# Projections of an mLSTM layer: two column blocks at a time, half of the k chunks by Strassen's seven products

## The chip, the core and the metric

The kernel runs on one core of one Trainium2 chip. Time is microseconds of device time for one execution; three runs of the kernel before took 1814.03 to 1814.68 us, median 1814.12. The engines that matter here are PE (TensorE, the matrix products), DVE (VectorE), ACT (ScalarE), and SP, whose queue issues the loads.

## The reference

One layer: RMSNorm, an input projection, a chunkwise mLSTM mixer with 8 heads, gates, an output projection. All inputs are float32, 256 rows of 4096 columns.

```
u = h @ w_in                                   # [256, 4096] @ [4096, 16400]
qk, v, og, z, ig, fg = split(u)                # 4096, 4096, 4096, 4096, 8, 8 columns
qk = silu(causal_dwconv(qk, conv_w, conv_b))   # 4 taps over time
... per head: hc = the gated matrix memory of q, k, v, normed by rows
y = hn * sigmoid(og) * silu(z)
out = x + y @ w_out                            # [256, 4096] @ [4096, 4096]
```

The two projections hold nearly all of the arithmetic. The mixer itself is small: a head has 256 rows, 256 columns of q and of k and 512 of v.

## The kernel before, in words

A float32 product is made of three passes of a faster format. `split` (L127) makes of an operand a high part (ACT, L129) and a low part (DVE, L130), and `matmul3` (L132) adds high by high, high by low and low by high into one PSUM bank: three products of 512 columns, about 0.4 us each in the profile and overlapping, for one k tile (128 of the 4096 rows of w) and one row tile (128 of the 256 rows).

`project` (L165) takes one block of 512 columns at a time. It walks over 8 chunks of 4 k tiles. A chunk of w is one load of 1 MB (L188, three buffers); two k tiles at a time are split (128x1024, tiles `wh`, `wl`, three buffers each) and give 12 products: 2 k tiles, 2 row tiles, 3 passes. x lies split in SBUF for the whole layer. Work on finished blocks (convolution, attention weights, values, gates) lies in `stages`, and one stage is issued behind each chunk of the blocks that follow. The first two blocks run together while x comes in. Blocks of a pair of heads come in the order og, z, og, z, q, k, v, v; then 9 blocks of w_out.

The order of instructions on each engine is the tile scheduler's, which also puts in the waits; a buffer is written again only when its last reader is done. Names in rows: `pj_o` is a PSUM tile of block o, `w_o` a raw load, `wh_o` and `wl_o` its high and low part.

## Time and profile before

| | |
|---|---|
| three runs, median | 1814.12 us |
| span of the profiled execution (its own time, first to last instruction) | 1812.6 us |
| PE busy | 1805.7 us, 100% of the span |
| DVE busy | 965.0 us, 53% |
| ACT busy | 848.8 us, 47% |
| loads and stores | 354.07 MB, mean 195 GB/s |

The span is 1.5 us under the median of the runs. Busy time of PE counts overlapping products once. Idle time of an engine off the chain of waits costs nothing.

### The profile page before, as it was taken

Reading aid. Unit: us, or ns where it says so; the run is one execution under the profiler, and the core shown is the slowest. Engines: PE = TensorE matmul, PEld = TensorE weight load, DVE = VectorE, ACT = ScalarE, POOL = GpSimd, SP = SyncE. Lnnn points to the kernel's source line nnn. Section 1 sums busy time; section 2 is a strip of 40 time slices with the busy share of each in tenths; the row PEclk is TensorE's granted clock in tenths of the full one; section 3 lists DMA queues with packets and bytes.
Section 4 is the critical chain, followed back from the end, with each engine's and each line's share of the span. In section 5 each row is a group of like instructions: output and inputs, shape, how many; then the busy total and the mean of one; then the engine's idle time right before and its main releaser. Section 6 shows DMA issues by size and latency. Waiting matters only on the chain.

```text
span 1812.6 us, 20931 instructions
## 1 busy us (share of the span) xinstructions
PE 1805.7 (100%) x8474; PEld 1510.6 (83%) x8474; DVE 965.0 (53%) x1133; ACT 848.8 (47%) x994; POOL 9.4 (1%) x24
## 2 busy tenths in 40 slices
...
GB/s 311 277 204 176 200 187 186 181 168 188 199 193 188 190 181 185 164 197 196 187 196 194 175 176 172 200 185 195 200 186 185 171 225 209 219 222 203 213 187 141
DMA packets 57089, 354.07 MB, mean 195 GB/s; under 512 B 6944, under 2 KB 8352, under 8 KB 18592
## 3 DMA queue, kind: packets, MB, share of 16 engines
...
HBM read 348.51 MB, written 4.19 MB: 195 GB/s over the span
## 4 chain that ended last, share of the span: by engine, by line
PE 99%; DMA 0%; SPq 0%; ACT 0%; DVE 0%; issue 0%
PE pj_v L135 7%; PE pj_o L136 6%; PE pj_o L134 6%; PE pj_o L135 6%; PE pj_v L136 6%; PE pj_v L134 6%; PE pj_og L135 6%; PE pj_og L134 6%; PE pj_og L136 6%; PE pj_z L135 6%; PE pj_z L136 6%; PE pj_z L134 6%; PE pj_k L135 3%; PE pj_k L134 3%; PE pj_k L136 3%; PE pj_q L135 3%
## 5 line engine op out<-in xcount | busy, mean ns | idle before, releaser
L130 DVE TENSOR_TENSOR wl_o<-w_o,wh_o 128x1024 fp32r<-128x1024 f32 x128 | 156.8, 1225 | 174.6 <-ACT wh_o L129 174.6
L129 ACT ACTIVATE wh_o<-w_o 128x1024 fp32r<-128x1024 f32 x128 | 135.8, 1061 | 206.8 <-PE pj_o L136 206.0
L130 DVE TENSOR_TENSOR wl_z<-w_z,wh_z 128x1024 fp32r<-128x1024 f32 x112 | 137.2, 1225 | 167.4 <-ACT wh_z L129 167.4
L130 DVE TENSOR_TENSOR wl_v<-w_v,wh_v 128x1024 fp32r<-128x1024 f32 x128 | 156.7, 1224 | 116.3 <-ACT wh_v L129 115.4
L135 PE MATMUL pj_o<-wl_o,yh 128*128 128x512 f32 (+1 forms) x576 | 210.5, 366 | 0.0
L136 PE MATMUL pj_o<-wh_o,yl 128*128 128x512 f32 (+1 forms) x576 | 210.5, 366 | 0.0
L130 DVE TENSOR_TENSOR wl_og<-w_og,wh_og 128x1024 fp32r<-128x1024 f32 x112 | 137.1, 1225 | 135.9 <-ACT wh_og L129 135.4
L129 ACT ACTIVATE wh_v<-w_v 128x1024 fp32r<-128x1024 f32 x128 | 135.6, 1060 | 154.6 <-PE pj_v L136 136.1
L135 PE MATMUL pj_v<-wl_v,xhi 128*128 128x512 f32 x512 | 202.4, 395 | 0.0
L136 PE MATMUL pj_v<-wh_v,xlo 128*128 128x512 f32 x512 | 199.9, 391 | 0.0
L129 ACT ACTIVATE wh_z<-w_z 128x1024 fp32r<-128x1024 f32 x112 | 118.8, 1061 | 169.5 <-PE pj_z L136 146.2
L129 ACT ACTIVATE wh_og<-w_og 128x1024 fp32r<-128x1024 f32 x112 | 118.8, 1060 | 160.7 <-PE pj_og L136 141.7
L134 PE MATMUL pj_o<-wh_o,yh 128*128 128x512 f32 (+1 forms) x576 | 193.3, 366 | 0.0
L134 PE MATMUL pj_v<-wh_v,xhi 128*128 128x512 f32 x512 | 183.7, 391 | 0.0
L135 PE MATMUL pj_og<-wl_og,xhi 128*128 128x512 f32 x448 | 175.0, 391 | 0.0
L136 PE MATMUL pj_og<-wh_og,xlo 128*128 128x512 f32 x448 | 174.4, 389 | 0.0
L135 PE MATMUL pj_z<-wl_z,xhi 128*128 128x512 f32 x448 | 174.3, 389 | 0.0
L136 PE MATMUL pj_z<-wh_z,xlo 128*128 128x512 f32 x448 | 174.3, 389 | 0.0
L134 PE MATMUL pj_og<-wh_og,xhi 128*128 128x512 f32 x448 | 158.3, 390 | 0.0
L134 PE MATMUL pj_z<-wh_z,xhi 128*128 128x512 f32 x448 | 156.1, 389 | 0.0
L136 PEld LDWEIGHTS pj_o<-wh_o,yl 128*128 128x128 f32 x576 | 108.7, 189 | 17.4
L134 PEld LDWEIGHTS pj_o<-wh_o,yh 128*128 128x128 f32 x576 | 108.7, 189 | 17.4
...
## 6 DMA issues: line engine op xcount, KB each, us to landing
...
w_o<-in_w_out SPq DMA_DIRECT2D x16, 512.0 KB, 3.5
```

The lines of the kernel that those rows point to most:

```text
L129: nc.scalar.activation(hi, src, AF.Copy)
L130: nc.vector.tensor_sub(lo, src, hi.bitcast(F32))
L134: nc.tensor.matmul(ps, a[0], b[0], start=first, stop=False)
L135: nc.tensor.matmul(ps, a[0], b[1], start=False, stop=False)
L136: nc.tensor.matmul(ps, a[1], b[0], start=False, stop=last)
```

## The change

Columns of w are now taken in pairs of blocks, 1024 columns by 256 rows: a 2x2 of blocks (two row tiles by two column blocks). In chunks 0, 2, 4 and 6 (`FAST`) the four k tiles are halved as well, and the 2x2 by 2x2 block product is formed by seven products of block sums instead of eight (the Winograd form). The sums on x's side (`F` in `build`, L190) are made once and kept; the sums on w's side are made anew for each pair, in place in the raw loads, on DVE (L246, L252, L255, L258). Each of the seven products `P1` to `P7` has its own PSUM bank for the whole pair. The other four chunks (`plain_steps`) go into four of these banks, so that the last combination, `combine` (L313), serves both: four copies on ACT (L321), seven sums of 128x512 on DVE (L322 to L328) at the end of each pair.

A step of a fast chunk has 6 products behind one split of 128x1024, a step of a plain chunk 12. A fast and a plain chunk together, which the steps interleave, are called a round below: 7 x 6 + 4 x 12 = 90 products, 11 splits and 4 sums of 128x1024; a pair has 4 rounds, and there are 19 pairs, 15 in w_in and 4 in w_out. In the kernel before, the same columns and chunks took 96 products and 8 splits.

Head 0's q, k, v and the gate columns (1040 columns) are projected plainly in a first part while x comes in; in its last chunks `build_x` (L219) loads x again and makes the 14 or 6 operand tiles of a chunk. Then follow the pairs oz0 (og and z of head 0), qkv1 (q, k, v of head 1), oz1, and so on to oz7, then o0 to o3. Finished heads are written to DRAM and read back during oz7 (`build_y`, L505), since the operands of x and of y share their place. The row norm goes into x's operands. Raw loads are 0.5 MB, seven buffers; `wh` and `wl` have three each, as before. The row sum of the weights, before a column of ones beside the values, is now 48 products of two columns.

```diff
-WARM = 8
-NPAIR = HEADS // 2
-OUT_BLOCKS = [NB] * 7 + [NB // 2] * 2
...
+FAST = (0, 2, 4, 6)
+ORDER = ("P1", "P3", "P2", "P5", "P7", "P6", "P4")
+TAGS = ORDER
...
+def block_pairs():
+    pairs = []
+    for h in range(HEADS):
+        if h:
+            pairs.append(("qkv", h, [(h * DQK, DQK), (QK + h * DQK, DQK)], [(O_V + h * DV, DV)]))
+        pairs.append(("oz", h, [(O_OG + h * DV, DV)], [(O_Z + h * DV, DV)]))
+    return pairs
...
+    def operand(name, src):
+        n = src.shape[-1]
+        hi = wpool.tile([P, RAW], F32R, name=f"wh_{name}", tag="whi")[:, :n]
+        lo = wpool.tile([P, RAW], F32R, name=f"wl_{name}", tag="wlo")[:, :n]
+        split(hi, lo, src)
+        return hi, lo
...
+    def load(name, w, off, n):
+        raw = wpool.tile([P, RAW], F32, name=f"w_{name}", tag="wraw", bufs=7)[:, :n]
+        nc.sync.dma_start(raw, source(w, off, n))
+        return raw
...
-    def project(name, w, off, widths, lhs, start=False, between=None, end=False):
-        """Column blocks of w side by side, from off on; returns the psum tiles of each."""
-        ps = [[pool.tile([P, NB], F32, name=f"pj_{name}_{b}_{t}", tag=tag)[:, :width] for t in range(NT)]
-              for b, (width, (pool, tag)) in enumerate(zip(widths, ((ps_pj, "pj"), (ps_n, "n"))))]
...
-                    hi = wpool.tile([P, SK, NB], F32R, name=f"wh_{name}_{b}_{c}_{k0}", tag="whi")
-                    lo = wpool.tile([P, SK, NB], F32R, name=f"wl_{name}_{b}_{c}_{k0}", tag="wlo")
-                    hi, lo = (u.rearrange("p a b -> p (a b)")[:, :n * width].rearrange("p (a b) -> p a b", a=n)
-                              for u in (hi, lo))
-                    split(hi, lo, raws[b].rearrange("p (a b) -> p a b", a=CK)[:, k0:k0 + n, :])
-                    order = [(j, t) for j in range(n) for t in range(NT)]
-                    for j, t in sorted(order, key=lambda jt: jt[1]) if end else order:
-                        matmul3(ps[b][t], a, (hi[:, j, :], lo[:, j, :]), c == 0 and k == 0,
-                                c == KT // CK - 1 and k == CK - 1)
...
+    def build(c, src):
+        if c in FAST:
+            flat = lhs_pool.tile([P, 2 * 7 * HK * P], F32R, name=f"lhs_{c}", tag=f"lhs{c}")
+            L = flat.rearrange("p (two s j t) -> p two s j t", two=2, s=7, j=HK)
+            a11, a12, a21, a22 = (src[:, j * HK:(j + 1) * HK, t * P:(t + 1) * P]
+                                  for t, j in ((0, 0), (0, 1), (1, 0), (1, 1)))
+            F = big(f"F_{c}", [P, 4, HK, P])
+            nc.vector.tensor_sub(F[:, 0], a21, a22)
+            nc.vector.tensor_sub(F[:, 3], a21, a11)
+            nc.vector.tensor_sub(F[:, 1], a11, F[:, 0])
+            nc.vector.tensor_sub(F[:, 2], a12, F[:, 1])
+            t0 = src[:, :, :P].rearrange("p (s j) t -> p s j t", s=2)
+            for s0, s1, v in ((0, 2, t0), (2, 3, a22.rearrange("p (s j) t -> p s j t", s=1)), (3, 7, F)):
+                for a in range(s0, s1):
+                    split(L[:, 0, a], L[:, 1, a], v[:, a - s0])
+            names = ("P1", "P2", "P4", "P5", "P6", "P3", "P7")
+            lhs[c] = {s: [[L[:, part, i, j, :] for part in range(2)] for j in range(HK)]
+                      for i, s in enumerate(names)}
...
+            flat = lhs_pool.tile([P, 2 * 3 * CK * P], F32R, name=f"lhs_{c}", tag=f"lhs{c}")
+            L = flat.rearrange("p (two s j t) -> p two s j t", two=2, s=3, j=CK)
+            F = big(f"F_{c}", [P, CK, P])
+            nc.vector.tensor_sub(F, src[:, :, :P], src[:, :, P:])
+            for i, v in enumerate((src[:, :, :P], src[:, :, P:], F)):
+                split(L[:, 0, i], L[:, 1, i], v)
+            lhs[c] = {s: [[L[:, part, i, j, :] for part in range(2)] for j in range(CK)]
+                      for i, s in enumerate(("T0", "T1", "D"))}
+    def build_x(c):
+        src = big(f"xn_{c}", [P, CK, T])
+        nc.sync.dma_start(src, xT[:, c * CK:(c + 1) * CK, :])
+        for j in range(CK):
+            k = c * CK + j
+            nc.vector.scalar_tensor_tensor(src[:, j, :], src[:, j, :], nw[:, k:k + 1], rstdB,
+                                           op0=OP.mult, op1=OP.mult)
+        build(c, src)
...
+    def fast_steps(name, w, off, c):
+        n = HK * NB
+        at = off + c * 4 * P * n
+        raw = {}
+        def made(s):
+            if s == "P1":
+                raw["11"] = load(f"{name}_{c}_11", w, at, n)
+            elif s == "P3":
+                raw["22"] = load(f"{name}_{c}_22", w, at + P * n, n)
+            elif s == "P2":
+                raw["21"] = load(f"{name}_{c}_21", w, at + 2 * P * n, n)
+            elif s == "P5":
+                if not DSUM:
+                    raw["12"] = load(f"{name}_{c}_12", w, at + 3 * P * n, n)
+                    nc.vector.tensor_add(raw["11"], raw["11"], raw["12"])
...
+                    nc.vector.tensor_add(raw["22"], raw["22"], raw["11"])
+            elif s == "P7":
+                if not DSUM:
+                    nc.vector.tensor_add(raw["12"], raw["12"], raw["22"])
+                if DSUM < 3:
+                    nc.vector.tensor_add(raw["21"], raw["21"], raw["11" if DSUM else "22"])
+            src = raw[{"P1": "11", "P3": "22", "P2": "21", "P5": "11", "P6": "11" if DSUM else "22",
+                       "P7": "22" if DSUM else "12", "P4": "21" if DSUM < 3 else "11"}[s]]
+            h = operand(f"{name}_{c}_{s}", src)
...
+            return [(s, [(lhs[c][s][j], b) for j, b in enumerate(by_k(h))])]
+        return [(c, lambda s=s: made(s), 1) for s in ORDER]
...
+    def plain_steps(name, w, off, c):
+        n = HK * NB
+        at = off + c * 4 * P * n
+        def made(i):
+            b = by_k(operand(f"{name}_{c}_{i}", load(f"{name}_{c}_{i}", w, at + i * P * n, n)))
+            return [(s, [(lhs[c][l][(i % 2) * HK + j], b[j]) for j in range(HK)])
+                    for s, l in ((("P3", "D"), ("P5", "T1")), (("P2", "T0"), ("P4", "T1")))[i // 2]]
+        return [(c, lambda i=i: made(i), 2) for i in range(4)]
...
+    def project_pair(name, w, off, between=None):
+        ps = {s: bank(f"{s}_{name}", s) for s in TAGS}
+        fast = [u for c in FAST for u in fast_steps(name, w, off, c)]
+        plain = [u for c in range(NCH) if c not in FAST for u in plain_steps(name, w, off, c)]
+        steps = sorted([((i + 0.5) / len(fast), u) for i, u in enumerate(fast)]
+                       + [((i + 1) / len(plain), u) for i, u in enumerate(plain)], key=lambda v: v[0])
+        total = len(fast) + 2 * len(plain)
+        uses = {s: len(FAST) * HK for s in TAGS}
+        for s in ("P2", "P3", "P4", "P5"):
+            uses[s] += (NCH - len(FAST)) * CK
+        seen = dict.fromkeys(TAGS, 0)
+        left = {c: 7 if c in FAST else 4 for c in range(NCH)}
+        done = popped = 0
+        for _, (c, make, cost) in steps:
+            for s, prods in make():
+                for a, b in prods:
+                    seen[s] += 1
+                    matmul3(ps[s], a, b, seen[s] == 1, seen[s] == uses[s])
+            left[c] -= 1
+            done += cost
+            if between is not None:
+                between(c if left[c] == 0 else None, done / total)
+            if done * NCH >= (popped + 1) * total:
+                popped += 1
+                if stages:
+                    stages.popleft()()
+        return ps
...
+    def combine(name, ps, xs=None):
+        A = work.tile([P, NT, NB], F32, name=f"A_{name}", tag="cA")
+        B = work.tile([P, NT, NB], F32, name=f"B_{name}", tag="cB")
+        p1 = work.tile([P, NB], F32, name=f"p1_{name}", tag="p1")
+        r7 = work.tile([P, NB], F32, name=f"r7_{name}", tag="r7")
+        tt = nc.vector.tensor_tensor
+        for dst, s in ((p1, "P1"), (B[:, 0], "P3"), (B[:, 1], "P5"), (r7, "P7")):
+            nc.scalar.activation(dst, ps[s], AF.Copy)
+        tt(A[:, 0], ps["P2"], p1, op=OP.add)
+        tt(B[:, 0], B[:, 0], B[:, 1], op=OP.add)
+        tt(p1, ps["P6"], p1, op=OP.subtract)
+        tt(r7, r7, p1, op=OP.add)
+        tt(B[:, 0], B[:, 0], p1, op=OP.add)
+        tt(B[:, 1], B[:, 1], r7, op=OP.add)
+        tt(A[:, 1], ps["P4"], r7, op=OP.subtract)
+        return A, B
...
+    def build_y(c):
+        src = big(f"yr_{c}", [P, CK, T])
+        nc.sync.dma_start(src, spill[c])
+        build(c, src)
...
+            for b in ((0,), (1, 2), (3, 4))[c - 5]:
+                build_x(b)
+    builds = deque((build_x, c) for c in range(5, NCH))
...
+    stages.extend([merged(gate_stages[0], conv[0]), merged(gate_stages[1], conv[1]), gate_stages[2],
+                   merged(gate_stages[3], hs[0])] + hs[1:])
...
+                f(b)
+            if n == len(pairs) - 1 and c is not None and c < HEADS - 1:
+                build_y(c)
+        ps = project_pair(f"{what}{h}", w_in, off, between)
+        off += D * 2 * NB
+        A, B = combine(f"{what}{h}", ps)
+        if what == "qkv":
+            for t in range(NT):
+                split(V[0][:, t, :], V[1][:, t, :], B[:, t, :])
+            hs, finish = head(h)
+            stages.extend(conv_qk(h, A) + hs)
+        else:
+            def gate_y(A=A, B=B, finish=finish):
+                sg = big("sg", [P, NT, NB])
+                nc.scalar.activation(A, A, AF.Sigmoid)
+                nc.scalar.activation(sg, B, AF.Sigmoid)
+                nc.vector.tensor_mul(B, B, sg)
+                nc.vector.tensor_mul(B, B, A)
+                finish(B)
+            gate_y()
+            stages.extend(turn(h))
...
-        ps, = project(f"o{n}", w_out, done * D, [width], ylist, end=n == len(OUT_BLOCKS) - 1)
...
+    for n in range(D // (2 * NB)):
+        cols = [slice((2 * n + i) * NB, (2 * n + i + 1) * NB) for i in range(2)]
+        ps = project_pair(f"o{n}", w_out, n * D * 2 * NB)
...
+        res = combine(f"o{n}", ps)
+        for i in (1, 0):
+            for t in range(NT):
+                nc.vector.tensor_add(xs[i][:, t, :], xs[i][:, t, :], res[i][:, t, :])
+                eng = nc.gpsimd if n < 3 else (nc.sync, nc.scalar)[t]
+                eng.dma_start(out[t * P:(t + 1) * P, cols[i]], xs[i][:, t, :])
```

Three places show how instructions move. First DVE, in the third block of w_out: before, its row holds only low parts (two to a load).

```order
L130 TENSOR_TENSOR wl_o2_0_1_0_11202<-w_o2_0_1_11199,wh_o2_0_1_0_11201 128x1024
L130 TENSOR_TENSOR wl_o2_0_1_2_11218<-w_o2_0_1_11199,wh_o2_0_1_2_11217 128x1024
L130 TENSOR_TENSOR wl_o2_0_2_0_11236<-w_o2_0_2_11233,wh_o2_0_2_0_11235 128x1024
L130 TENSOR_TENSOR wl_o2_0_2_2_11252<-w_o2_0_2_11233,wh_o2_0_2_2_11251 128x1024
L130 TENSOR_TENSOR wl_o2_0_3_0_11270<-w_o2_0_3_11267,wh_o2_0_3_0_11269 128x1024
L130 TENSOR_TENSOR wl_o2_0_3_2_11286<-w_o2_0_3_11267,wh_o2_0_3_2_11285 128x1024
```

Now the same engine in the third pair of w_out, at the start of a round (chunks 4 and 5; `P1` to `P7` are steps of the fast chunk 4, `_5_0` and `_5_1` the first two of the plain chunk 5; rows of L246, L255, L252 and L258 are the in-place sums).

```order
L135 TENSOR_TENSOR wl_o2_4_P1_13670<-w_o2_4_11_13667,wh_o2_4_P1_13669 128x1024
L135 TENSOR_TENSOR wl_o2_4_P3_13682<-w_o2_4_22_13679,wh_o2_4_P3_13681 128x1024
L246 TENSOR_TENSOR w_o2_4_11_13667<-w_o2_4_11_13667,w_o2_4_12_13721 128x1024
L255 TENSOR_TENSOR w_o2_4_12_13721<-w_o2_4_12_13721,w_o2_4_22_13679 128x1024
L135 TENSOR_TENSOR wl_o2_5_0_13694<-w_o2_5_0_13691,wh_o2_5_0_13693 128x1024
L252 TENSOR_TENSOR w_o2_4_22_13679<-w_o2_4_22_13679,w_o2_4_11_13667 128x1024
L135 TENSOR_TENSOR wl_o2_4_P2_13712<-w_o2_4_21_13709,wh_o2_4_P2_13711 128x1024
L135 TENSOR_TENSOR wl_o2_4_P5_13725<-w_o2_4_11_13667,wh_o2_4_P5_13724 128x1024
L258 TENSOR_TENSOR w_o2_4_21_13709<-w_o2_4_21_13709,w_o2_4_22_13679 128x1024
L135 TENSOR_TENSOR wl_o2_5_1_13737<-w_o2_5_1_13734,wh_o2_5_1_13736 128x1024
```

Between the low part of P3 and that of the second plain step stand four sums that were not there.

The second place is DVE where pair o2 begins: the sums that finish pair o1 (`A_o1`, `p1_o1`, `r7_o1`, `B_o1`; L322 to L326) and its first addition to x (L623) stand among the low parts of the new pair.

```order
L135 TENSOR_TENSOR wl_o2_0_P3_13374<-w_o2_0_22_13371,wh_o2_0_P3_13373 128x1024
L246 TENSOR_TENSOR w_o2_0_11_13359<-w_o2_0_11_13359,w_o2_0_12_13413 128x1024
L322 TENSOR_TENSOR A_o1_13329<-P2_o1_12702,p1_o1_13331 128x512
L255 TENSOR_TENSOR w_o2_0_12_13413<-w_o2_0_12_13413,w_o2_0_22_13371 128x1024
L135 TENSOR_TENSOR wl_o2_1_0_13386<-w_o2_1_0_13383,wh_o2_1_0_13385 128x1024
L324 TENSOR_TENSOR p1_o1_13331<-P6_o1_12705,p1_o1_13331 128x512
L623 TENSOR_TENSOR xo_1_0_13323<-xo_1_0_13323,A_o1_13329 128x512
L135 TENSOR_TENSOR wl_o2_0_P2_13404<-w_o2_0_21_13401,wh_o2_0_P2_13403 128x1024
L252 TENSOR_TENSOR w_o2_0_22_13371<-w_o2_0_22_13371,w_o2_0_11_13359 128x1024
L135 TENSOR_TENSOR wl_o2_0_P5_13417<-w_o2_0_11_13359,wh_o2_0_P5_13416 128x1024
L325 TENSOR_TENSOR r7_o1_13332<-r7_o1_13332,p1_o1_13331 128x512
L326 TENSOR_TENSOR B_o1_13330<-B_o1_13330,p1_o1_13331 128x512
```

Five instructions of 128x512 have come in ahead of the low part of the second plain step, which is the second row behind these.

The third is PE in the round of the first place: the last products of P5, then the second plain step (`_5_1`, banks P3 and P5).

```order
L141 MATMUL P5_o2_13355<-wh_o2_4_P5_13724,lhs_4_11744 128x512
L139 MATMUL P5_o2_13355<-wh_o2_4_P5_13724,lhs_4_11744 128x512
L140 MATMUL P5_o2_13355<-wl_o2_4_P5_13725,lhs_4_11744 128x512
L141 MATMUL P5_o2_13355<-wh_o2_4_P5_13724,lhs_4_11744 128x512
L139 MATMUL P3_o2_13353<-wh_o2_5_1_13736,lhs_5_11784 128x512
L139 MATMUL P5_o2_13355<-wh_o2_5_1_13736,lhs_5_11784 128x512
L139 MATMUL P7_o2_13356<-wh_o2_4_P7_13753,lhs_4_11744 128x512
L140 MATMUL P3_o2_13353<-wl_o2_5_1_13737,lhs_5_11784 128x512
L141 MATMUL P3_o2_13353<-wh_o2_5_1_13736,lhs_5_11784 128x512
```

Two high products of the plain step and one of P7 stand ahead of the first product (L140) that asks for the low part `wl_o2_5_1`.

## Rows read from the trace of the kernel before

**Rows 1.** The page: busy time of the engines, and the chain that ended last.
```profile
PE 1805.7 (100%) x8474; PEld 1510.6 (83%) x8474; DVE 965.0 (53%) x1133; ACT 848.8 (47%) x994; POOL 9.4 (1%) x24
...
PE 99%; DMA 0%; SPq 0%; ACT 0%; DVE 0%; issue 0%
```

**Rows 2.** Windows: stretch, busy us (instructions) by engine, clock, DMA share, GB/s.
```profile
12.00:20.00 8.00, 8.00 (x36) 6.54 (x36) 6.35 (x12) 5.98 (x12) 0.00 (x0) 0.98 1.04 361
800.00:900.00 100.00, 100.00 (x443) 82.83 (x442) 47.88 (x41) 41.29 (x41) 0.00 (x0) 1.00 0.54 191
```

**Rows 3.** Timeline inside block z: start us, us, engine, line, operation, idle before.
```profile
799.52 1.06 ACT L129 ACTIVATE wh_z<-w_z 128x1024 fp32r<-128x1024 f32 x1 [1.66 <-PE pj_z L136]
...
801.82 0.39 PE L136 MATMUL pj_z<-wh_z,xlo 128*128 128x512 f32 x1
...
802.24 1.06 ACT L129 ACTIVATE wh_z<-w_z 128x1024 fp32r<-128x1024 f32 x1 [1.66 <-PE pj_z L136]
803.34 1.23 DVE L130 TENSOR_TENSOR wl_z<-w_z,wh_z 128x1024 fp32r<-128x1024 f32 x1 [1.50 <-ACT wh_z L129]
```

**Rows 4.** Timeline, ACT, last block of 256 columns.
```profile
1789.17 1.06 ACT L129 ACTIVATE wh_o<-w_o 128x1024 fp32r<-128x1024 f32 x1 [1.87 <-PE pj_o L136]
1792.05 1.06 ACT L129 ACTIVATE wh_o<-w_o 128x1024 fp32r<-128x1024 f32 x1 [1.82 <-PE pj_o L136]
```

**Rows 5.** Groups by line, DVE: count, busy us, mean ns of one, idle before.
```profile
L130 DVE TENSOR_TENSOR wl_o<-w_o,wh_o 128x1024 fp32r<-128x1024 f32 x128 | 156.8, 1225 | 174.6 <-ACT wh_o L129 174.6
L289 DVE SCALAR_TENSOR_TENSOR acc<-pt,cw,acc 128x254 f32<-128x254 f32 x32 | 15.4, 481 | 1.1
L430 DVE TENSOR_TENSOR G<-G,sgo 128x512 f32<-128x512 f32 x16 | 10.4, 683 | 0.1
L130 DVE TENSOR_TENSOR wl_first<-w_first,wh_first 128x512 fp32r<-128x512 f32 x8 | 5.4, 690 | 5.9 <-ACT wh_first L129 5.9
```

**Rows 6.** Timeline, DVE, where it ran without a gap.
```profile
22.57 3.50 DVE L130 TENSOR_TENSOR wl_first<-w_first,wh_first 128x1024 fp32r<-128x1024 f32 x3 [0.47 <-ACT wh_first L129]
28.87 3.25 DVE L162 SCALAR_TENSOR_TENSOR xlo<-xT,nw,xhi 128x256 fp32r<-128x256 f32 x8
...
1501.61 1.28 DVE L462 TENSOR_TENSOR o<-pj_o,o 128x512 f32<-128x512 f32 x2
```

**Rows 7.** Timeline, DVE, two that depend on each other (L430 reads what L428 wrote).
```profile
99.47 0.74 DVE L428 SCALAR_TENSOR_TENSOR G<-pj_first,rstd,G 128x512 f32<-128x512 f32 x1
100.25 0.69 DVE L430 TENSOR_TENSOR G<-G,sgo 128x512 f32<-128x512 f32 x1
```

**Rows 8.** The page: loads, KB each, median us from issue to landing.
```profile
w_o<-in_w_out SPq DMA_DIRECT2D x16, 512.0 KB, 3.5
w_first<-in_w_in SPq DMA_DIRECT2D x6, 512.0 KB, 8.4
```

**Rows 9.** The start: PE's timeline, and a window over it.
```profile
9.61 0.63 PE L136 MATMUL pj_first<-wh_first,xlo 128*128 128x512 f32 x1
10.03 0.63 PE L135 MATMUL pj_first<-wl_first,xhi 128*128 128x512 f32 x1
...
5.00:12.00 7.00, 4.70 (x13) 3.45 (x14) 2.54 (x5) 3.02 (x6) 0.00 (x0) 0.78 0.93 274
```

**Rows 10.** Timeline, the end.
```profile
1808.96 0.28 PE L136 MATMUL pj_o<-wh_o,yl 128*128 128x256 f32 x1
1809.28 0.42 DVE L462 TENSOR_TENSOR o<-pj_o,o 128x256 f32<-128x256 f32 x1 [1.01 <-PE pj_o L136]
```

More of the change, by code (lines that the diff above doesn't have):

```diff
@@ L300, in mlstm_layer @@
[L300 to L316 removed]
+        return take, [forget, sums, maxima, floor]
@@ new lines, in mlstm_layer, with head, decay @@
+    V = [lhs_pool.tile([P, NT, DV], F32R, name=f"v{part}") for part in range(2)]
+    y = {}
+    def head(h):
+        qT, kT = qk
+        A = [work.tile([P, 3 * P], F32R, name=f"A{part}_{h}", tag=f"A{part}") for part in range(2)]
+        E = work.tile([P, 3 * P], F32, name=f"E_{h}", tag="E")
+        spans = ((0, 0, T, 0), (1, T, 3 * P, P))
+        r = small.tile([P, NT], F32, name=f"r_{h}", tag="r")
+        ss = small.tile([P, NT], F32, name=f"ss_{h}", tag="ssh")
+        s2 = small.tile([P, NT], F32, name=f"s2_{h}", tag="s2", bufs=2)
+        def decay():
+            pM = misc(f"pM_{h}", [P, T])
@@ L350, in values, with rows @@
+        def rows():
+            pq = misc(f"pq_{h}", [P, NT, 2])
+            for t in range(NT):
+                mm = [(a, part) for a, _ in terms[t] for part in range(2)]
+                for n, (a, part) in enumerate(mm):
+                    nc.tensor.matmul(pq[:, t, :], A[part][:, a * P:(a + 1) * P], onesr, start=n == 0,
+                                     stop=n == len(mm) - 1)
+            nc.scalar.activation(r, pq[:, :, 0], AF.Abs)
             nc.vector.tensor_max(r, r, gate["enm"][:, :, h])
@@ L378, in head, with last @@
-        return [weights, values, turn]
-    ylhs = {}
-    def split_y(c):
-        hi = act_in.tile([P, CK, T], F32R, name=f"yh_{c}", tag=f"hi{c}")
-        lo = act_in.tile([P, CK, T], F32R, name=f"yl_{c}", tag=f"lo{c}")
-        split(hi, lo, yT[:, c * CK:(c + 1) * CK, :])
-        ylhs[c] = (hi, lo)
-    lhs = []
-    off = 0
-    G, qk, sgo = {}, {}, {}
-    blocks = column_blocks()
-    for n, (what, who, spans) in enumerate(blocks):
-        width = sum(w for _, w in spans)
-        def between(c, n=n):
-            if n == 0 and c >= 4:
-                for t in range(NT):
-                    row_squares(t, c - 4)
-            if n == len(blocks) - 1 and c >= 2:
-                split_y(c - 2)
-        if n == 0:
-            both = project("first", w_in, off, [width, width], lhs, True, between)
+        def last():
+            values(1)
+            scale()
```

404 lines of the change are left out of this document (195 added, 209 removed).

## The prediction

> **What bounds the kernel now.** I read the engine totals first, then the chain of waits: PE is busy 1805.7 of 1812.6 us and holds 99% of the chain, DVE 965.0 and ACT 848.8 [rows 1]. So the time is a sum of products, and the windows say that they run at the full clock (1.00) with the loads at half of the stretch [rows 2]. Inside a block the timeline gives the price of a product: ACT begins a new high part every 2.72 us (799.52, 802.24), in which PE does 12 products of 512 columns, so 0.2267 each; with 256 columns 24 in 2.88 us, 0.120 each [rows 3, 4]. The same rows give the hand-offs: a product that starts at 801.82 and takes 0.39 releases ACT at 802.24, ACT's 1.06 releases DVE at 803.34; 0.03 to 0.05 us each. DVE's durations are in the groups [rows 5]. What counts here is its rate when it never waits: three of 128x1024 end to end in 3.50 us, so 1.13 from start to start; eight of 128x256 in 3.25 (0.40); two of 128x512 in 1.28 (0.60 start to start, 0.68 alone) [rows 6].
>
> **What PE saves.** By the order, products of 512 columns in the projections fall from 7296 to 7032 (a round of 90 where there were 96): 264 x 0.2267 = 59.8. Projections of 256 columns fall from 576 to 192: 384 x 0.120 = 46.1. Values go from 144 of 256 to 72 of 512 columns: 17.3 - 16.3 = 1.0. The 48 products of two columns are nowhere in the trace; between 0 and 0.12 each (a 256), I take 0.05, 2.4. Together -104.5: 1812.6 - 104.5 = 1708 is PE's own floor, in the profiled execution's time. The runs' median lies 1.5 above that span.
>
> **What DVE gets.** A round has 11 low parts and 4 in-place sums of 128x1024: 15 x 1.13 = 17.0 beside 90 x 0.2267 = 20.4 on PE. The trace has no in-place sum of 1024; a 512 in place costs 683 ns where a split costs 690, so I give it a split's 1.13 [rows 5]. It isn't less, as the two stream alike, and at most 1.265 where its input was written by the instruction just before: of two such of 512, the second starts 0.78 after the first, 0.04 behind its end [rows 7], and 1.225 + 0.04 is 1.265. So DVE has room on average, and ACT (11 x 1.06 of 20.4) more. The question is whether three `wh`/`wl` buffers let DVE use its room.
>
> They don't quite. Four sums stand ahead of the low part of the second plain step (`_5_1` in the order), among the low parts. From the start of the low part of P3 DVE goes through eight instructions, then that ninth: 8 x 1.13 + 0.135 (one dependent pair) + 1.225 = 10.4 us. Only then can PE go on. ACT's high part of the next round's P3 needs a buffer that PE leaves 39 products later: 38 x 0.2267 + 0.39 = 9.0. ACT's 1.06 and two hand-offs (0.07) close the circle: 10.4 + 9.0 + 1.13 = 20.6 us, just above PE's 20.4. So PE and DVE are both critical in every round: 76 rounds x 0.2 = 15. More important: whatever else DVE must do inside those 10.4 us comes on top in full, while behind the second plain step there are only some 1 to 3 us of room a round (9.0 + 1.13 less six to eight instructions).
>
> **What is put inside.** At each of 18 seams the order puts four sums of the last pair (L322, L324, L325, L326) there: 4 x 0.62 = 2.5, plus 0.3 for what stands behind and overflows: 18 x 2.8 = 50. Behind an og/z pair follow two products of 128x1024 of `gate_y` and the last sums, 2 x 1.13 + 0.6 less 1.1 of room: 1.7, eight times, 14. Three seams of w_out have an addition to x inside: 3 x 0.6 = 2. Seams: 66.
>
> Head work (convolution, values, norms) is near 20 us of DVE a head: 965.0 less 628 low parts of 1.225 is 196, less x's preparation (30), over 8. Spread over 8 rounds it exceeds the room by some 5 us a head; PE's small products, 7 us a head (1805.7 less all counted products is 41, by 8, and 2 of values), run while PE waits anyway. I set the two against each other: 0, bound +-35 for seven heads.
>
> Pair oz0 also builds x's operands for three chunks. A plain chunk: 4 x 0.40 + 0.6 + 3 x 0.6 = 4.0; a fast one: 15 instructions of 256, 6.0; so 14. DVE 4 x 17.0 + 14 + 20 = 102 against PE's 81.6 + 7.1 = 88.7: +14, and 2 for loads that landed in 8.4 where the queue was full [rows 8]: +16. Pair oz7 builds seven chunks of y (four of 11 x 0.40, three of 2.4: 25): 68 + 25 + 20 = 113 against 88.7, less 3.6 charged above: +21. The first part makes operands of five chunks (26 of DVE by the same counts) while x lands; between 0 and all of it shows, I take 5, nearer to nothing, since DVE is half idle there; and its banks are handed to `P1` to `P7` behind copies, +2. At the end seven sums and four additions, ten of them one behind another at 0.65, stand behind the last product, where before one addition of 0.42 stood [rows 10]: 6.5, and a store twice as large: +7.
>
> Sum: 15 + 66 + 0 + 16 + 21 + 7 + 7 = 132. 1708 + 132 = 1840 in the profile's time, 1841.5 as a median: slower by 27 us (1.5%). With each loss a third smaller or larger and head work at its bounds: 1815 to 1885 for this case alone; I would put it at 1818 to 1870 more narrowly.
>
> **Rivals.** (a) *The buffers absorb it.* Seven raw buffers and three split ones let PE run ahead in the light half of a round and fall back in the heavy one, so that only the longer sum of a stretch counts. For it: 15 x 1.13 is 3.4 us under PE's 20.4, and nothing on the circle but the 0.2 is really late. Against it: ACT follows PE by exactly one freed buffer before (its idle time is ended by PE) [rows 3, 4], so there is no stock of split tiles. Then the time is 1708 + 14 (oz0) + 20 (oz7) + 7 (end) = 1749, 1750 as a median; with half of my losses 1775. Faster. It decides where the four seam sums cost under half of their 2.5 us and the y builds under 20.
>
> (b) *The fourth load is late.* `w_.._12` can be issued only when a buffer of the round before is free, and its data opens the chain of four sums. From the order its issue has 6.5 us in a plain round and 4.5 in one packed with head work (some 26). The trace lands 512 KB in 3.5 us, or at 361 GB/s streams one in 1.45 [rows 2, 8]; in the crowded start it took 8.4. At 3.5 nothing is late, which is what I count. With two loads in front, 3.5 + 2 x 1.45 = 6.4, it is 1.9 late in each packed round: 49 more, 1891.
>
> (c) *DVE doesn't keep its dense rate.* If each of the sums counts as dependent: 4 x 0.135 x 76 = 41 more, 1881. If every one of 8 instructions in the circle starts only at the other's end (1.225 for 1.13): 8 x 0.095 x 76 = 58, 1899. Against it: the dense stretch runs below its single durations, 3.50 for 3 x 1.225 [rows 5, 6].
>
> The second price is what a rule of the Trainium skill would give (VectorE: DVE Perf Modes, section "The DRAIN you can't avoid"): the next operation doesn't begin until the pipe of the last has emptied. The dense stretch here contradicts it for independent instructions, since 3.50 is less than 3.68; the same section adds that an operation that isn't held starts earlier, which agrees.
>
> (d) *The clock falls.* In the first 7 us PE is busy 4.70 and the window's clock is 0.78; products there start 0.425 apart, the lower level (1.2 GHz) [rows 9]. If the waits of a packed round brought that back, a round would cost 90 x (0.425 - 0.2267) = 18 us at worst; with 5 or 6 in each of 26 packed rounds 143 more: 1985. Against it: the waits I expect are 2 to 4 us in 24, and in 800 to 900 the clock holds at 1.00 [rows 2].
>
> The Trainium skill warns of this (TensorE: Matmul & The Clock Gate, "HAM oscillation"): idle gaps between bursts bring TensorE back to half rate. The start here agrees that a PE with pauses stands at the lower level; no row of before has pauses later on.
>
> That fewer products are made than counted is excluded by the order, and that none are saved likewise.
>
> **Numbers.** Forecast (slower, 1818 to 1870) with its tails: 0.47. (a): 0.38, between 1745 and 1810, of which a sliver reaches no change. (b) 0.08, (c) 0.04, (d) 0.03. A measurement of this kernel tells 0.2% from no change, so "same" is 1810.5 to 1817.7: 0.05, taken half from (a), half from the forecast. Faster 0.36, slower 0.59. The range that leaves out 2 in 10: the lower end cuts (a) at 1765 (about 0.1 lies below), the upper at 1890 leaves out (d), half of (b) and of (c).
>
> **What would show it.** DVE busy 1610 to 1720 us (1155 instructions of 128x1024 at 1.13 to 1.225, 133 sums at 0.62, head work 160, operands of x and y 67), about 90%; PE near 1705 busy of 1840. In the chain, PE and DVE mixed, with L246 to L258 and L135 in it. In the inner rounds of o0 to o3, ACT's P3 parts 20.6 us apart, in the first round after a seam about 23.5 to 24, in oz0 and oz7 about 26. PE idle, waiting for `wl` of the second plain step (L140), at every seam. The clock at 1.00 throughout. Wrong if the rounds come at 20.4 and the first ones too: then (a). If sums of L246 wait for SP's queue: (b). If 128x1024 instructions of a dense run start over 1.2 apart: (c). The largest single doubt is the seam term: 66 us rest on the order of four sums, and if DVE is early there because PE's small products fell elsewhere, half of it goes.

## The result: slower, 1845.3 us, by the circle that was forecast

The changed kernel took 1845.3 us (median of four runs, 1844.5 to 1845.8), the kernel before 1814.4 beside it: 1.0168 times as long, 95% interval 1.0154 to 1.0183. (Below, the numbers in brackets behind a time are this ratio to the kernel before, measured beside it, and its interval.) The forecast was 1841.5. The profiled execution spans 1844.1 us.

The page of the changed kernel, to be held against [rows 1]: engine totals, and the chain.

```profile
PE 1773.2 (96%) x7804; PEld 1410.7 (77%) x7804; DVE 1654.5 (90%) x1882; ACT 1135.5 (62%) x1303; POOL 12.1 (1%) x29
...
PE 69%; DVE 19%; issue 7%; ACT 3%; DMA 2%; SPq 0%; DVEq 0%; ACTq 0%
```

PE has 670 products fewer, and yet the span grew: the chain, 99% PE before, is now 69% PE and 19% DVE. An inner round (the third of pair o2) on DVE's timeline (start, us, engine, line, operation, idle before):

```profile
1703.46 2.60 DVE L135 TENSOR_TENSOR wl_o_P<-w_o,wh_o_P 128x1024 fp32r<-128x1024 f32 x2 [0.15 <-ACT wh_o_P L134]
1705.97 1.22 DVE L246 TENSOR_TENSOR w_o<-w_o,w_o 128x1024 f32<-128x1024 f32 x1
1707.23 1.23 DVE L255 TENSOR_TENSOR w_o<-w_o,w_o 128x1024 f32<-128x1024 f32 x1
1708.37 1.22 DVE L135 TENSOR_TENSOR wl_o<-w_o,wh_o 128x1024 fp32r<-128x1024 f32 x1
1709.51 1.22 DVE L252 TENSOR_TENSOR w_o<-w_o,w_o 128x1024 f32<-128x1024 f32 x1
1710.64 2.35 DVE L135 TENSOR_TENSOR wl_o_P<-w_o,wh_o_P 128x1024 fp32r<-128x1024 f32 x2
1712.91 1.22 DVE L258 TENSOR_TENSOR w_o<-w_o,w_o 128x1024 f32<-128x1024 f32 x1
1714.05 1.22 DVE L135 TENSOR_TENSOR wl_o<-w_o,wh_o 128x1024 fp32r<-128x1024 f32 x1
...
1719.01 1.23 DVE L135 TENSOR_TENSOR wl_o_P<-w_o,wh_o_P 128x1024 fp32r<-128x1024 f32 x1 [1.47 <-ACT wh_o_P L134]
...
1725.68 1.23 DVE L135 TENSOR_TENSOR wl_o_P<-w_o,wh_o_P 128x1024 fp32r<-128x1024 f32 x1
```

The second of the two in the first row is P3's low part; it starts 1.14 before L246, at 1704.83. The last row is P3's of the next round: 20.85 later. From the one start to the end of the second plain step's low part (1715.27) DVE runs without a gap, 10.44 us (10.4 forecast). Behind it stand gaps ended by ACT, and ACT in turn waits for PE to give a buffer back. PE over the point where that low part is handed over, then ACT's high part of the next round's P3:

```profile
1715.08 0.39 PE L139 MATMUL P_o<-wh_o_P,lhs 128*128 128x512 f32 x1
1715.32 0.50 PE L140 MATMUL P_o<-wl_o,lhs 128*128 128x512 f32 x1
1715.65 0.39 PE L141 MATMUL P_o<-wh_o,lhs 128*128 128x512 f32 x1
1715.88 0.39 PE L139 MATMUL P_o<-wh_o,lhs 128*128 128x512 f32 x1
...
1724.58 1.06 ACT L134 ACTIVATE wh_o_P<-w_o 128x1024 fp32r<-128x1024 f32 x1 [0.31 <-PE P_o L141]
```

L140 is the product that needs it, and the one after starts 0.33 behind: a wait of 0.1 a round that, being shorter than a product, never shows as idle time. ACT's high part starts 9.26 behind L140 and ends 0.04 before DVE's next P3 at 1725.68: this closes the circle. What the forecast did not have is the step between ordinary products: 0.23 (0.2306 on average over the whole run, mostly between 0.224 and 0.238), where before it was 0.2267 wherever no head work came between [rows 3], 0.2270 on average. (Averages here and below leave out steps over 0.245, which hold a wait, a slower clock or a small product.)

The first round of the same pair, where o1's combination stands:

```profile
1659.74 1.23 DVE L135 TENSOR_TENSOR wl_o_P<-w_o,wh_o_P 128x1024 fp32r<-128x1024 f32 x1 [0.15 <-ACT wh_o_P L134]
1660.88 1.22 DVE L246 TENSOR_TENSOR w_o<-w_o,w_o 128x1024 f32<-128x1024 f32 x1
1662.02 0.68 DVE L322 TENSOR_TENSOR A_o<-P_o,p_o 128x512 f32<-128x512 f32 x1
...
1664.89 0.68 DVE L324 TENSOR_TENSOR p_o<-P_o,p_o 128x512 f32<-128x512 f32 x1
1665.49 0.68 DVE L623 TENSOR_TENSOR xo<-xo,A_o 128x512 f32<-128x512 f32 x1
...
1669.49 0.69 DVE L325 TENSOR_TENSOR r_o<-r_o,p_o 128x512 f32<-128x512 f32 x1
1670.09 0.69 DVE L326 TENSOR_TENSOR B_o<-B_o,p_o 128x512 f32<-128x512 f32 x1
1670.70 1.22 DVE L258 TENSOR_TENSOR w_o<-w_o,w_o 128x1024 f32<-128x1024 f32 x1
1671.83 1.22 DVE L135 TENSOR_TENSOR wl_o<-w_o,wh_o 128x1024 fp32r<-128x1024 f32 x1
```

The same path takes 13.31 here, not one gap in it, and the round 23.68 (rounds are counted from one P3's low part to the next). Such a place, where a pair begins and the last one is combined, is called a seam. Windows (us, then busy us and instructions of PE, PEld, DVE, ACT, POOL, clock, DMA share, GB/s) of an inner round, this first round, oz0 and oz7:

```profile
1704.80:1725.70 20.90, 20.90 (x92) 16.80 (x91) 17.60 (x16) 11.69 (x11) 0.00 (x0) 1.00 0.60 203
1659.70:1683.40 23.70, 22.03 (x92) 16.60 (x91) 23.23 (x25) 11.69 (x12) 2.17 (x4) 1.00 0.59 193
110.50:215.00 104.50, 93.98 (x392) 71.43 (x393) 97.83 (x133) 65.63 (x87) 0.00 (x0) 0.97 0.50 168
1374.90:1485.70 110.80, 98.55 (x413) 74.65 (x411) 108.50 (x162) 73.20 (x107) 0.00 (x0) 0.98 0.55 190
```

DVE is busy 108.5 of 110.8 us in oz7. The end, to be held against [rows 10]: five 512 sums and four additions follow the last product (1835.18) one behind another.

```profile
1835.18 0.40 PE L141 MATMUL P_o<-wh_o,lhs 128*128 128x512 f32 x1
...
1838.80 1.28 DVE L623 TENSOR_TENSOR xo<-xo,B_o 128x512 f32<-128x512 f32 x2
1840.00 0.68 DVE L623 TENSOR_TENSOR xo<-xo,A_o 128x512 f32<-128x512 f32 x1
```

### The profile page after: what moved, and what is told of

It reads as the page before. It is cut to its first block, busy times and chain, and to the rows that moved or that the text cites. A ratio compares the mean times of both kernels' runs of the same rounds, so it can differ in the third digit from the quotient of the medians.

```text
span 1844.1 us, 21723 instructions
## 1 busy us (share of the span) xinstructions
PE 1773.2 (96%) x7804; PEld 1410.7 (77%) x7804; DVE 1654.5 (90%) x1882; ACT 1135.5 (62%) x1303; POOL 12.1 (1%) x29
## 4 chain that ended last, share of the span: by engine, by line
PE 69%; DVE 19%; issue 7%; ACT 3%; DMA 2%; SPq 0%; DVEq 0%; ACTq 0%
PE P_qkv L140 9%; PE P_qkv L141 9%; PE P_qkv L139 9%; PE P_oz L140 9%; PE P_oz L141 8%; PE P_oz L139 8%; PE P_o L140 4%; PE P_o L141 4%; PE P_o L139 4%; DVE wl_oz_P L135 2%; DVE wl_oz L135 2%; DVE lhs L135 1%; DVE w_oz L246 1%; DVE wl_o_P L135 1%; DVE wl_o L135 1%
## 5 line engine op out<-in xcount | busy, mean ns | idle before, releaser
L134 ACT ACTIVATE wh_oz_P<-w_oz 128x1024 fp32r<-128x1024 f32 x224 | 237.6, 1061 | 109.0 <-PE P_oz L141 91.7
L135 DVE TENSOR_TENSOR wl_oz_P<-w_oz,wh_oz_P 128x1024 fp32r<-128x1024 f32 x224 | 270.8, 1220 | 20.2 <-ACT wh_oz_P L134 18.4
L135 DVE TENSOR_TENSOR wl_qkv_P<-w_qkv,wh_qkv_P 128x1024 fp32r<-128x1024 f32 x196 | 237.1, 1221 | 43.4 <-ACT wh_qkv_P L134 40.7
L134 ACT ACTIVATE wh_qkv_P<-w_qkv 128x1024 fp32r<-128x1024 f32 x196 | 208.1, 1062 | 82.5 <-PE P_qkv L141 73.2
L140 PE MATMUL P_oz<-wl_oz,lhs 128*128 128x512 f32 x512 | 205.1, 401 | 11.4 <-DVE wl_oz L135 10.3
L139 PE MATMUL P_oz<-wh_oz,lhs 128*128 128x512 f32 x512 | 190.7, 401 | 18.4 <-ACT wh_oz L134 17.4
L141 PE MATMUL P_oz<-wh_oz,lhs 128*128 128x512 f32 x512 | 201.6, 394 | 0.0
L140 PE MATMUL P_qkv<-wl_qkv,lhs 128*128 128x512 f32 x448 | 178.7, 399 | 4.0 <-DVE wl_qkv L135 4.0
L140 PE MATMUL P_oz<-wl_oz_P,lhs 128*128 128x512 f32 x448 | 179.4, 401 | 1.1 <-DVE wl_oz_P L135 1.1
L139 PE MATMUL P_oz<-wh_oz_P,lhs 128*128 128x512 f32 x448 | 178.6, 403 | 2.0 <-ACT wh_oz_P L134 2.0
L141 PE MATMUL P_oz<-wh_oz_P,lhs 128*128 128x512 f32 x448 | 176.7, 394 | 0.0
L141 PE MATMUL P_qkv<-wh_qkv,lhs 128*128 128x512 f32 x448 | 175.7, 392 | 0.0
L135 DVE TENSOR_TENSOR wl_oz<-w_oz,wh_oz 128x1024 fp32r<-128x1024 f32 x128 | 156.1, 1219 | 21.1 <-ACT wh_oz L134 21.1
L139 PE MATMUL P_qkv<-wh_qkv,lhs 128*128 128x512 f32 x448 | 162.1, 395 | 4.8 <-ACT wh_qkv L134 4.8
L135 DVE TENSOR_TENSOR wl_o_P<-w_o,wh_o_P 128x1024 fp32r<-128x1024 f32 x112 | 135.3, 1222 | 24.6 <-ACT wh_o_P L134 23.1
L135 DVE TENSOR_TENSOR wl_qkv<-w_qkv,wh_qkv 128x1024 fp32r<-128x1024 f32 x112 | 136.6, 1220 | 21.8 <-ACT wh_qkv L134 21.7
L140 PE MATMUL P_qkv<-wl_qkv_P,lhs 128*128 128x512 f32 x392 | 155.2, 396 | 0.0
L139 PE MATMUL P_qkv<-wh_qkv_P,lhs 128*128 128x512 f32 x392 | 152.8, 394 | 1.5 <-ACT wh_qkv_P L134 1.5
L141 PE MATMUL P_qkv<-wh_qkv_P,lhs 128*128 128x512 f32 x392 | 153.5, 391 | 0.0
```

The costliest lines, as they stand in the source:

```text
L134: nc.scalar.activation(hi, src, AF.Copy)
L135: nc.vector.tensor_sub(lo, src, hi.bitcast(F32))
L139: nc.tensor.matmul(ps, a[0], b[0], start=first, stop=False)
L140: nc.tensor.matmul(ps, a[0], b[1], start=False, stop=False)
L141: nc.tensor.matmul(ps, a[1], b[0], start=False, stop=last)
```

## The experiments

Theory 1 is the forecast's circle: nine DVE instructions from P3's low part to the second plain step's, 39 products, ACT's high part; what stands among the nine costs in full. Its rival, theory 2: the sum of DVE's work sets the pace. Theory 3 came from the trace: the slower products are the whole loss.

**Where the work stands, not how much.** Two runs take the same two sums' worth off DVE, at different places. Inside the nine:

```diff
-        tt(r7, r7, p1, op=OP.add)
+        tt(r7[:, :8], r7[:, :8], p1[:, :8], op=OP.add)
-        tt(B[:, 0], B[:, 0], p1, op=OP.add)
+        tt(B[:, 0, :8], B[:, 0, :8], p1[:, :8], op=OP.add)
```

> The changed kernel with two of the seven sums of each pair (L325, L326) made over 8 columns instead of 512, which leaves part of the combination out. At the seams these two stand between the low part of P3 and that of the second plain step; otherwise order and banks stay. Theory 1 (the circle of DVE's nine instructions, 39 products and ACT's high part sets a round, and what stands inside those nine comes on top in full): first rounds of pairs shorter by 2 x 0.56 = 1.1 us, 18 times: 20 us less, 1825. Theory 2 (the sum of DVE's work sets the pace): 19 x 2 x 0.56 = 21 less as well. Theory 3 (PE's own slower products are the whole loss): no change, 1845.

Outside them, the same cut to L323 and L327:

```diff
-        tt(B[:, 0], B[:, 0], B[:, 1], op=OP.add)
+        tt(B[:, 0, :8], B[:, 0, :8], B[:, 1, :8], op=OP.add)
...
-        tt(B[:, 1], B[:, 1], r7, op=OP.add)
+        tt(B[:, 1, :8], B[:, 1, :8], r7[:, :8], op=OP.add)
```

> The changed kernel with two other sums of the seven (L323, L327) over 8 columns, which leaves part of the combination out. They stand outside the stretch from the low part of P3 to that of the second plain step. DVE has exactly as much less to do as with L325 and L326 cut down. Theory 1 (only what stands inside the stretch counts): 0 to 4 us less, 1841 to 1845. Theory 2 (the sum of DVE's work counts): 21 less, 1824. Theory 3 (PE's products): 1845.

Measured: outside 1844.3 (1.0172, 1.0155 to 1.0189), 1 us less than the changed kernel where theory 2 wants 21. Inside 1856.9 (1.0233, 1.0218 to 1.0249), 12 us more, where theories 1 and 2 both wanted some 20 less and theory 3 no change. The rounds tell why. In pair o2's first round of that run the two stand for 0.17 us each:

```profile
1675.88 1.22 DVE L135 TENSOR_TENSOR wl_o_P<-w_o,wh_o_P 128x1024 fp32r<-128x1024 f32 x1 [0.15 <-ACT wh_o_P L134]
...
1685.63 0.17 DVE L325 TENSOR_TENSOR r_o<-r_o,p_o 128x8 f32<-128x8 f32 x1
1685.71 0.17 DVE L326 TENSOR_TENSOR B_o<-B_o,p_o 128x8 f32<-128x8 f32 x1
1685.79 1.23 DVE L258 TENSOR_TENSOR w_o<-w_o,w_o 128x1024 f32<-128x1024 f32 x1
1686.92 1.23 DVE L135 TENSOR_TENSOR wl_o<-w_o,wh_o 128x1024 fp32r<-128x1024 f32 x1
```

The path is 12.27 long (1675.88 to 1688.15) against 13.31, and the first rounds of the qkv pairs fell from 24.24 to 23.18 us, of oz pairs from 23.37 to 22.83, of o1 to o3 from 23.68 to 22.88: some 14 in all, as theory 1 has it (1.1 a seam) for the qkv pairs and half to three quarters of it elsewhere. But the scheduler, which counts with its own times, set head work in another order: the third rounds of oz1 to oz6 grew from 23.4 to 28 (six times 4.6 is 28), where DVE now waits for PE in front of a queue of low parts; the row shows 1.45 of it.

```profile
910.62 0.56 DVE L439 SCALAR_TENSOR_TENSOR E<-pS,E 128x384 f32<-128x384 f32 x1 [1.45 <-PE pS L141]
```

So the total of that run is no evidence; the seams in it are, for the qkv pairs in full. In the outside run the same seams of o2 and o3 kept their 23.6, those of oz grew (23.37 to 24.78) about as much as rounds behind them shrank, and those of qkv fell (24.24 to 23.70) about as much as the rounds behind them grew: the order moved here as well. That 21 us less of DVE's work give back 1 speaks against theory 2; the next run decides.

**The circle opened.** With a fourth buffer (raw loads give up one of seven):

```diff
-        hi = wpool.tile([P, RAW], F32R, name=f"wh_{name}", tag="whi")[:, :n]
+        hi = wpool.tile([P, RAW], F32R, name=f"wh_{name}", tag="whi", bufs=4)[:, :n]
...
-        raw = wpool.tile([P, RAW], F32, name=f"w_{name}", tag="wraw", bufs=7)[:, :n]
+        raw = wpool.tile([P, RAW], F32, name=f"w_{name}", tag="wraw", bufs=6)[:, :n]
...
```

> The changed kernel with four buffers each for high and low parts in place of three, and six for raw loads in place of seven. DVE has just as much to do. Theory 1: a high part then waits for a step of PE that ended some nine products earlier, the circle falls to about 9.3 + 7.1 + 1.1 = 17.5 us, below PE's 20.75; the four sums of a seam (2.5) fit beside it; inner rounds 20.75, first rounds of pairs near 21, some 60 us less in all: 1785 (1770 to 1805). Theory 2 (the sum of DVE's work sets the pace): 1845. Theory 4 (the raw buffer that is given up makes loads late): slower than 1845.

Measured 1783.3 (0.9825, 0.9810 to 0.9840): 62 less than with three, 2 from the forecast, with DVE at the same work. Its page:

```profile
PE 1746.9 (98%) x7804; PEld 1417.8 (80%) x7804; DVE 1638.4 (92%) x1882; ACT 1124.1 (63%) x1303; POOL 12.1 (1%) x29
...
PE 83%; DVE 11%; issue 2%; DMA 2%; ACT 0%; SPq 0%; DVEq 0%; ACTq 0%
```

DVE is busy for a larger share of the time (92% for 90%) and the kernel is faster: this is the decisive run against theory 2. One part of the expectation missed: first rounds of o1 to o3 still take 23.05 between P3's low parts and not 21, but the rounds behind them are shorter than PE's 20.75 (19.4, 20.6 and 20.7 in o2), so that the pair's four take 83.7, near 4 x 20.75. The fourth buffer lets a heavy round be made up for. So rival (a) of the prediction ("the buffers absorb it") is what happens with four buffers, not with three.

**Less DVE work.** Without the four in-place sums (L246, L252, L255 and L258 deleted); and with two fast chunks:

```diff
-FAST = (0, 2, 4, 6)
+FAST = (0, 4)
```

> The changed kernel without the four in-place sums on w's side (the steps split the raw blocks as they were loaded, so the products are of other numbers; their count, the loads, the splits and the combination stay). Theory 1 (the circle): its DVE part falls from 10.4 to about 6 us, rounds become PE's own 90 x 0.2306 = 20.75, seams cost nothing, oz0 and oz7 little: 7104 products at 0.2306 make PE's floor 1708 + 28 = 1736, with start and end 1757 (1745 to 1775). Theory 2 (the sum of DVE's work): nothing of it would be left to hold PE back either, the same time. Theory 3 (slower products are the whole loss): 1845 less nothing.

> The changed kernel with two fast chunks of eight (0 and 4) in place of four: 12 products more in each of 19 pairs, and 14 instructions of 128x1024 less on DVE in each. Theory 1: rounds become PE's own; 1736 + 228 x 0.2306 = 1789, with start, end and what is left of oz7 1806 (1798 to 1818): faster than the changed kernel and than the kernel before. Theory 3 (products are slower, and DVE doesn't matter): 1845 + 52 = 1897.

Measured 1783.6 (0.9830, 0.9814 to 0.9847) and 1831.9 (1.0096, 1.0081 to 1.0111): the sums do cost some 62 us, but both runs are 26 us above what theory 1 gave, and outside its ranges, by the same amount. A window of the first run over the first part shows one piece of it:

```profile
20.00:108.00 88.00, 80.92 (x494) 72.39 (x492) 64.66 (x120) 55.45 (x91) 0.00 (x0) 0.96 0.82 291
```

PE pauses 7 us there, and the clock is 0.96, which takes some 3.5 more (an estimate, 0.04 x 88). In all of that run PE stood idle 37 us (1 before its first instruction, 10 in the first part, 6.5 in oz0, 5 in oz7, 5 elsewhere, 9 behind the last product), where the expectation had counted 21 on top of a floor that holds the kernel before's own 7: that is 9 of the 26, the clock some 3.5. The rest is not taken apart here. Fewer fast chunks are no way out: with two, the kernel is still slower than before.

**Two of the sums made by loads that add** (`DSUM = 1`; it then pairs blocks otherwise than w is laid out, so its output is of other numbers):

> The changed kernel with two of the four sums made by DMAs that add into SBUF as they load (issued from POOL's queue), two left on DVE. Theory 1, if these loads land in time: the stretch from P3 to the second plain step is some 2.3 us shorter, inner rounds 20.75, seams about 1.5 longer than that: 1790 (1775 to 1810). Rival: a load that adds costs more to issue or to land than 4 us, and what waited for DVE waits for it: 1845 to 1950.

Measured 2004.7 (1.1046, 1.1030 to 1.1063): the rival, and slower than its range. What waits is ACT, for landings:

```profile
ACT wh_qkv_P L134 <- DMA w_qkv<-in_w_in: 108.5, 27, 5.9
...
w_qkv<-in_w_in POOLq DMA_DIRECT2D x56, 512.0 KB, 7.4
```

(waited for: us in all, times, longest; then issues, KB, median us to landing.) An adding load can start only when its block has been split, and landed 5.7 to 7.4 us later (medians of its three groups). The clock fell as well: PE stood idle 174 us, and the mean granted clock was 0.968, where the changed kernel's is 0.993; at most some 50 of the 159 us lost are that (an estimate, 0.032 x 2001 less 0.007 x 1844).

**The slower products.** First idea: tiles that begin 32 bytes past a multiple of 64 are read faster. The changed kernel, and the kernel before, moved up by 32 bytes (`pad = const.tile([P, 8], ...)` ahead of all tiles):

> The changed kernel with every SBUF tile moved up by 32 bytes (an unused tile of 8 columns ahead of all others); nothing else moves in any engine's order. In the kernel before, products of 512 columns start 0.2267 us apart, to the nanosecond; in the changed kernel 0.2306 on average, between 0.224 and 0.236. In the kernel before w's tiles begin 32 bytes past a multiple of 64, in the changed kernel at multiples of 128. Theory A (the place of the tiles sets it): products return to 0.2267, inner rounds from 20.86 to about 20.6 us, the whole by 7000 x 0.0039 less what DVE then holds back, about 1822 (1815 to 1830). Theory B (the interval comes from something else, as the pauses of PE or the busier DVE): 1845, products still 0.2306.

> The kernel before with every SBUF tile moved up by 32 bytes, so that w's tiles begin at multiples of 64; the order is unchanged on every engine. Theory A (the place of the tiles sets the interval of products): 0.2306 in place of 0.2267, 7296 x 0.0039 = 28 us more and some for the shorter products, 1843 or a little over. Theory B: 1814, products at 0.2267.

Measured 1846.6 (1.0178) and 1814.65 (1.0000, 0.9990 to 1.0009); products at 0.2307 and 0.2270 on average, as they were. Theory A fell. Products were 0.2306 without DVE's in-place sums too, so they aren't the cause either. What repeated in the trace was the sequence of intervals, and it went with which of the three buffers a step used. Those lie 4224 bytes apart, at differing places modulo 512; before, they lay 4096 apart, at one place (by the tiles' sizes in the code; the traces hold no addresses). Hence:

```diff
-        hi = wpool.tile([P, RAW], F32R, name=f"wh_{name}", tag="whi")[:, :n]
+        hi = wpool.tile([P, 1152], F32R, name=f"wh_{name}", tag="whi")[:, :n]
...
```

> The changed kernel with the tiles of high and low parts 4608 bytes apart in place of 4224 (a multiple of 512) and 128 bytes further on, so that all that PE reads in a projection, w's parts and x's, begins at the same place modulo 512, as in the kernel before (there 160, here 128). No engine's order changes. In the changed kernel w's parts lie at four places modulo 512, and rounds that use the three buffers in the same turn show the same sequence of intervals, others another. Theory A2 (tiles at differing places keep products from their shortest interval): 0.2267 returns, inner rounds 10.4 + 9.0 + 1.1 = 20.6 for 20.86, 1824 (1815 to 1832). Theory B (something else): 1845, 0.2306.

Measured 1837.3 (1.0124, 1.0109 to 1.0139). PE in pair o2:

```profile
1697.07 0.39 PE L141 MATMUL P_o<-wh_o,lhs 128*128 128x512 f32 x1
1697.29 0.39 PE L140 MATMUL P_o<-wl_o,lhs 128*128 128x512 f32 x1
1697.52 0.39 PE L141 MATMUL P_o<-wh_o,lhs 128*128 128x512 f32 x1
1697.75 0.39 PE L139 MATMUL P_o<-wh_o,lhs 128*128 128x512 f32 x1
1697.97 0.39 PE L140 MATMUL P_o<-wl_o,lhs 128*128 128x512 f32 x1
```

0.2267 is back as the usual step (the four shown take 0.90; 0.2277 on average), but only 8 us come off, where 21 were expected: the inner round is 20.76, above PE's own 20.4 and above the 20.6 expected of the circle. So theory 3 falls. The converse, in the kernel before, whose PE sets the pace alone: low parts 128 bytes further on than high parts, `pad` of 32 columns between them.

> The kernel before with the low parts' tiles 128 bytes further on than the high parts' (an unused tile between them; two small tiles elsewhere share room to pay for it): high parts and x at 64 modulo 512, low parts at 192. The order of products is the same but for one place. Theory A2 (differing places modulo 512 keep products from their shortest interval, whatever else the engines do): one moving operand in three changes place, twice each three products; 0.2267 becomes 0.228 to 0.231 and the whole 1825 to 1845. Theory B (it takes the changed kernel's own arrangement): 1814.

Measured 1833.8 (1.0105, 1.0090 to 1.0120): 19 us slower with the same products, splits and loads. ACT's high parts, 12 products apart as in [rows 3]:

```profile
797.96 1.06 ACT L129 ACTIVATE wh_z<-w_z 128x1024 fp32r<-128x1024 f32 x1 [1.69 <-PE pj_z L136]
800.70 1.06 ACT L129 ACTIVATE wh_z<-w_z 128x1024 fp32r<-128x1024 f32 x1 [1.69 <-PE pj_z L136]
```

2.74 instead of 2.72; between 800 and 900 us it is the step from L135 (which reads the low part) to L136 (the high part) that takes 0.234, all others 0.226 to 0.227. In other stretches other steps are long as well; the average over the run is 0.2299.

**Both mends together:** four buffers, tiles 4096 bytes apart at one place modulo 512; the wide first loads split one k tile at a time.

> Four buffers for high and low parts (six for raw loads) as in the run that took 1783, and their tiles 4096 bytes apart at the same place modulo 512 as x's operands; for that the wider part of the first loads is split one k tile at a time (16 more short splits while x comes in). Theory A2: PE sets the pace in that run, so 7000 products shorter by 0.004 us come off in full: 1755 (1748 to 1768). Theory B: 1783.

Measured 1762.5 (0.9713, 0.9697 to 0.9729): 83 less than the changed kernel, 52 less than before: faster than both. Products are 0.2267 apart again (0.2272 on average). It misses 1755 by 7; in pair o2 the four rounds take 83.2 us for 81.6 of products, so not all of PE's gain comes through. DVE is at 93% there; that this is why is not shown. A last run moved the sums on x's and y's side to POOL:

> The run that took 1762.5 with the sums on x's and y's side (F, made once per chunk) on POOL instead of DVE: 5 x (4 or 1) of them in the first part and oz0, 7 chunks in oz7. If those stretches are held back by DVE's sum of work: oz7 up to 8 us shorter, oz0 3: about 1754 (1750 to 1760). Rival: POOL takes longer for a sum than DVE and the operands of a chunk come later, or slows DVE down beside it: 1762 to 1775.

Measured 1776.8 (0.9791, 0.9775 to 0.9808): the rival, a little over its range. POOL took 4.0 and 4.6 us (means of four and three; once, for head 7, 1.6) for a sum of 512 columns, DVE 0.68, and the operands that are made of it wait. Pair oz7 grew from 100.5 to 109.1 us.

```profile
L213 POOL TENSOR_TENSOR F<-xn 128x512 f32<-128x512 f32 x4 | 16.0, 4001 | 50.0 <-DVE xn L224 45.9 <-ACT af L353 4.1
L213 POOL TENSOR_TENSOR F<-yr 128x512 f32<-128x512 f32 x3 | 13.8, 4600 | 8.4 <-DVE lhs L135 5.7 <-DVE wl_oz_P L135 2.6
```

## Why the prediction was right, step by step

| stretch | forecast, from its terms | measured |
|---|---|---|
| DVE's path inside a round | 10.4 | 10.44 |
| inner round | 20.6 | 20.86 |
| first round of o2 (20.6 + 2.8 + 0.6) | 24.0 | 23.68 |
| head 4, two pairs (170.3 + 1.6 + 5.6 + 1.7) | 179.2 | 178.7 |
| oz0 (88.7 + 16 + 0.8) | 105.5 | 104.5 |
| oz7 (88.7 + 21 + 3.6) | 113.3 | 110.8 |
| behind the last product, against before | +7 | +5.1 (8.5 for 3.4) |
| DVE busy | 1610 to 1720 | 1654.5 |

The circle, the seams and the builds are right in mechanism and near in size. The run with four buffers shows that it is the buffers and not the sum of DVE's work, and the one with L323 and L327 cut points the same way. "In full" for what stands inside is shown for the seams of qkv pairs (1.06 of 1.1) and not for the others (0.54 and 0.80). The dense rate held for in-place sums too (L252 to what follows it: 1709.51 to 1710.64, 1.13), and the one that writes what the instruction before it reads starts 1.26 behind it (1705.97 to 1707.23; 1.265 forecast). So rival (c) falls, and with it, for instructions that don't wait for each other, the rule of the Trainium skill that was quoted beside it.

The mis-sized term is the price of a product: 0.2267 was taken over from [rows 3], and 7104 products at 0.2306 make PE's floor 28 us higher. An inner round came out 0.26 longer: 39 of its 90 products stand on the circle (0.15), and the wait of 0.1 behind L140 was not in the sum. The total still came out near, because other terms had been put too high: the head, which rounds of 20.86 should have brought to 181, took 178.7 (2.6 less, seven times; the setting of head work against small products is the softest of its terms, but the runs don't take them apart), oz7 2.5, the end 2. So the 4 us between forecast and result are partly luck. "PE near 1705 busy" failed with it (1773.2): products that start late by less than their own length count as busy.

Rival (b) was nearly absent: L246 waited for a load three times, 1.8 us in all. Of (d) there is a little: the clock was 1.00 in the steady rounds, but 0.94 in 20 to 109 us, 0.97 in oz0, 0.98 in oz7.

```profile
20.00:109.00 89.00, 82.23 (x499) 73.68 (x497) 65.11 (x120) 55.90 (x92) 0.00 (x0) 0.94 0.81 288
```

That is at most some 11 us in all, an estimate (0.06 x 89, 0.03 x 104.5, 0.02 x 110.8), so "the clock at 1.00 throughout" was wrong in those stretches. The Trainium skill (TensorE: Matmul & The Clock Gate, "HAM oscillation — how this bites in real kernels") says that idle gaps between bursts do this. The stretches with most of PE's pauses (7 us in the window above, 11 in oz0, 12 in oz7) are the ones with the lower clock here, which agrees; the short waits of the rounds did not bring it down (1.00 in the first round of o2, with 1.7 us of them).
